# A decoder layer in three-pass fp32r: two chunks of branch B side by side, branch A's inputs loaded sooner, sums of x later in VectorE's order

## The chip, the cores and the metric

One core of a Trainium2 chip runs the whole program in one launch. The metric is the device time in microseconds (us) of that core, as a median over runs. In the profile PE is TensorE (PEld its weight loads), DVE is VectorE, ACT is ScalarE, POOL is GpSimd and SP is SyncE, the engine that issues the DMAs here.

## The reference

The kernel computes one layer of a hybrid decoder for 1024 positions of width 1024 (f32), and a final norm. Cut to the shape of it (the gains and the head reshapes left out):

```python
x = x + 0.5 * swiglu_1(rms(x))                  # width 2816
h = rms(x)
q, f, i, og, pool, gate_a, gate_b = split(h @ w_in)
o   = hgrn2(q, f, i)                            # 8 heads, chunkwise recurrence
y_a = (rms_per_head(o) * silu(og)) @ w_branch_a       # branch A, 1024 x 1024
m   = pool_means(pool) - pool, through pool_w and a scale   # windows 2, 4, 8, 16
y_b = m @ w_branch_b                                  # branch B, 512 x 1024
y   = sigmoid(gate_a) * y_a + sigmoid(gate_b) * y_b
x = x + y @ w_out
x = x + 0.5 * swiglu_2(rms(x))
x = x + sigmoid(rms(x) @ w_ple_gate) * rms(p @ w_ple)
out = rms(x)
```

The change touches the three products with w_branch_b, w_branch_a and w_out.

## The kernel before

**Products.** Every operand of a product is split in two fp32r numbers, hi (cast on ACT, L120) and lo (the remainder, subtracted on DVE, L121). `mm3` issues three matmuls for each product: hi by hi (L159), lo by hi (L160) and hi by lo (L161), each 128x512 into one PSUM bank. The large products go by a seven-product scheme on quarters of the matrices, so operands are also sums and differences of quarters: of weights on POOL (L90, L93), of activations on DVE (L84).

**Order.** A tile framework orders the instructions of each engine ahead of time from the traced program. Within an engine the order is then fixed, and an instruction that waits holds all behind it. `load` (L151) and `store` (L155) are DMAs, all issued by SP, in its order. `behind[0]` names an SP instruction that every load traced from then on is put behind, on SP; `latest[0]` is the load or store traced last. PSUM has tags with 3 (pA), 1 (pB), 1 (pC) and 3 (aux) banks; SBUF tiles come from tagged pools, so that a tile can be written only when the one that had its place has been read.

**Branch B.** `branch_b(j)` makes rows chunk j of y_b: it loads 512 columns' weights rw, splits them to wb, loads the gate gb, does 12 matmuls for each half of the positions into a pA bank (named yb), multiplies by the gate on DVE (L87) and stores to yb_dram. Chunk 0 is done earlier, among the heads; chunks 1 to 7 come here, one after another. Their right operands mh and ml (`m_parts`, four groups of the pool channels) stay in the tag "a" until the last chunk has read them.

**Branch A.** `load_act(i)` loads a quarter of branch A's input (o_dram) as two tiles b1 and b2 and splits it into the operands x0, x3, xT1 and xT3; the tiles lie in the tag "a", too. It is called behind chunks 1, 3, 5 and 7 of branch B. The loop over j = 0, 2, 4, 6 then runs `out_pair`: it loads two quarters of weights, ra and rb, makes wah/wal from ra, wsh/wsl and wth/wtl from sums of both, and wd, and does the seven products. `done` loads a gate and a part of y_b into gy, multiplies, adds, and stores y to y_dram.

**Output product.** `tok` runs over items (product i, half q), with the sides made ahead of the item that uses them: the left operands y (from y_dram) two items ahead, the right ones wo (weights rB, or stored differences rT, rN) four ahead. When a product is done, `read` adds its four banks to x on DVE (L81). Afterwards the norm of the second feed-forward block squares the rows of x on ACT (L220).

Of the kernel before, what the change touches and what calls it, by code (L numbers as in the profile page):

```python
# [16 lines left out]
P = 128  # L17
# [3 lines left out]
KC = D // P  # L21
# [16 lines left out]
def hybrid_block(ctx: ExitStack, tc: tile.TileContext, a: dict, out: bass.AP):  # L38
# [47 lines left out]
    def mul(o, x, y):  # L86
        nc.vector.tensor_tensor(o, x, y, ALU.mult)  # L87
# [414 lines left out]
    ORDER = (1, 2, 5, 6, 3, 7, 4)  # L502
    TOK_TAGS = ("pA", "pA", "pA", "pB"), ("pC", "aux", "aux", "aux")

    def tok(items, lhs, rhs, read, between={}, ahead=2):

# [2 lines left out]
        def operands(of, i, qs):  # L511
            return sum((of(i, q) for q in (qs if isinstance(qs, tuple) else (qs,))), [])

        sides = {lhs: ([], 2), rhs: ([], ahead)}

        def trace(of, at):
            if at < len(items):
                sides[of][0].append(operands(of, *items[at]))

        for at in range(ahead):  # L520
            for of, (_, n) in sides.items():
# [2 lines left out]
        for at, (i, q) in enumerate(items):  # L524
# [6 lines left out]
            for j in range(4):  # L531
                if start:
                    banks[line][j] = bank(TOK_TAGS[line][j])
                ps = banks[line][j]
                c = slice(j * P, (j + 1) * P)
                for k, ((ah, al), (bh, bl)) in enumerate(zip(ls, rs)):
                    mm3(ps, ah[:, c], al[:, c], bh, bl, start and k == 0, last and k == len(ls) - 1)
                if last:
                    read(i, j, ps)
            if (i, q) in between:  # L540
                between[i, q]()

# [647 lines left out]
    def branch_b(j):  # L1190
        r = load(t_("w", "rw")[:, :HALF], a["w_branch_b"][j])
        wh, wl = hilo_half(r, "w", "wb")
        for half, cols in enumerate((L, R)):
# [6 lines left out]
            mul(gb, ps, gb)  # L1200
            store(yb_dram[j][half], gb)

    with tc.manual_schedule(engines={nc.tensor.engine}):
        for h in range(HEADS):
            its = more[h]() if h in more else (v_pair(h + 1), qf_pair(h + 1), og_pair(h + 1))
            among(its, head(h), (66 if h == 7 else 3 * PAIR + 9 * (h in (0, 2))))
        while turns:
            turns.pop(0)()
    behind[0] = og_last[0]

    act_a = new_act()

    def load_act(i):

        b1, b2 = t_("q", "b1"), t_("q", "b2")
        for b, half in ((b1, 0), (b2, 1)):
            for c, at in ((L, 2 * i), (R, 2 * i + 1)):
                load(b[:, c], o_dram[at][half])
        b11, b21, b12, b22 = b1[:, L], b1[:, R], b2[:, L], b2[:, R]

        def put(names, hl):
# [9 lines left out]
        sub(b21, b21, b22)  # L1231
        put(("T1", "N4"), hilo(b1, "a", "xT1"))
        put(("T3", "T2"), hilo(b2, "a", "xT3"))

    for j in range(1, KC):
        steps(branch_b(j))
        if j % 2:
            load_act(j // 2)
    behind[0] = latest[0]


# [68 lines left out]
    def read(i, j, ps):  # L1310
# [8 lines left out]
    rows_2, go_2 = to_next(2)  # L1319
    tok([(i, q) for q in range(2) for i in (1, 2)] + [(i, q) for i in ORDER[2:] for q in range(2)],  # L1320
        *tok_sides(y_of, a["w_out"], wo_dram), read,
        {(3, 1): lambda: rows_2(x), (7, 1): lambda: go_2(x)}, 4)
    act = rest_of(x)
    behind[0] = None

# [174 lines left out]
```

## Time and profile before

| what | value |
|---|---|
| median of 3 runs | 2363.16 us (2357.85 to 2366.03) |
| the profiled execution's own time | 2363.49 us |
| span of the profiled execution | 2361.8 us |
| mean granted clock | 0.992 of full speed |
| TensorE busy | 2312.1 us, 98% |
| VectorE busy | 1469.4 us, 62% |
| ScalarE busy | 983.9 us, 42% |
| GpSimd busy | 447.1 us, 19% |

Times inside the program are counted from the start of the span, so the profiled execution has 1.7 us outside of it. The granted clock is the share of TensorE's full clock (2.4 GHz) that the chip gave it; 0.50 is the lower level, 1.2 GHz. The number in square brackets at the end of a timeline row is how long the engine stood idle ahead of that instruction, and what ended the idle time.

### The profile page before, as it was taken

What the parts mean: (1) busy time and instruction counts of PE and PEld (TensorE: products, weight loads), DVE (VectorE), ACT (ScalarE), POOL (GpSimd) and SP (SyncE); (2) the same over time, 40 slices, a digit from 0 to 9 for tenths busy, and PEclk for the clock granted to TensorE, in tenths of its full rate; (3) what the DMA queues carried; (4) which work ended last, traced back from release to release, by engine and by line L of the source; (5) the groups of instructions that cost most, each with busy time, mean ns of one, the idle gap of its engine ahead of it and who ended that gap; (6) DMA issues with size and microseconds to landing.
All of it is one profiled execution on the core that took longest, in us unless ns stands there. A gap on an engine that the chain in (4) does not pass through costs nothing.

```text
span 2361.8 us, 29424 instructions
## 1 busy us (share of the span) xinstructions
PE 2312.1 (98%) x11058; PEld 1918.6 (81%) x11058; DVE 1469.4 (62%) x2024; ACT 983.9 (42%) x1536; POOL 447.1 (19%) x387
## 2 busy tenths in 40 slices
PE   8999999999999999999999999999999999999998
PEld 6778888888887888788888887877787888888886
DVE  5655555467657765666566666677555644568457
ACT  6434333333555333334433443337333433334555
POOL 1322222200012132122212202101422232100001
PEclk9999999999999999999999999999999999999999
DMA  4344444483332232232232366752344523664245
GB/s 177 137 151 169 153 174 142 147 339 110 135 112 76 76 104 72 78 106 72 83 100 87 99 206 221 252 223 106 102 161 170 201 93 112 231 241 135 80 165 183
DMA packets 137503, 341.19 MB, mean 144 GB/s; under 512 B 15632, under 2 KB 16656, under 8 KB 137360
## 3 DMA queue, kind: packets, MB, share of 16 engines
q1 hardware_dynamic: 137360, 339.31, 41.4%
q8 instruction: 87, 1.43, 0.3%
q14 instruction: 56, 0.46, 0.1%
HBM read 233.86 MB, written 105.38 MB: 144 GB/s over the span
## 4 chain that ended last, share of the span: by engine, by line
PE 80%; DVE 6%; DMA 5%; issue 4%; POOL 2%; ACT 2%; SPq 1%; POOLq 0%; DVEq 0%; ACTq 0%
PE pA L159 13%; PE pA L161 13%; PE pA L160 13%; PE pB L159 6%; PE pB L161 6%; PE pB L160 6%; PE aux L1035 4%; PE pC L161 3%; PE pC L159 3%; PE pC L160 3%; PE aux L161 2%; PE aux L160 2%; PE aux L159 2%; DMA rb<-in_ffn_w_dram 1%; PE tr L268 1%
## 5 line engine op out<-in xcount | busy, mean ns | idle before, releaser
L90 POOL TENSOR_TENSOR s<-rb 128x512 f32<-128x512 f32 x74 | 99.5, 1345 | 755.6 <-DMA rb<-in_ffn_w_dram 318.5
L121 DVE TENSOR_TENSOR wtl<-rb,wth 128x1024 fp32r<-128x1024 f32 x74 | 90.6, 1225 | 158.3 <-ACT wth L120 158.3
L120 ACT CAST wsh<-s 128x1024 fp32r<-128x1024 f32 x74 | 77.8, 1051 | 224.8 <-POOL s L93 188.4
L93 POOL TENSOR_TENSOR rb<-ra,s 128x512 f32<-128x512 f32 x74 | 97.8, 1322 | 331.8 <-DVE wd L121 331.8
L121 DVE TENSOR_TENSOR wal<-ra,wah 128x1024 fp32r<-128x1024 f32 x74 | 91.6, 1239 | 100.2 <-PE pC L160 64.4
L121 DVE TENSOR_TENSOR wsl<-s,wsh 128x1024 fp32r<-128x1024 f32 x74 | 90.9, 1229 | 100.7 <-ACT wsh L120 100.6
L120 ACT CAST wth<-rb 128x1024 fp32r<-128x1024 f32 x74 | 77.6, 1049 | 180.8 <-POOL rb L93 180.8
L120 ACT CAST gh<-gr 128x1024 fp32r<-128x1024 f32 x84 | 81.9, 981 | 143.7 <-PE aux L160 86.6
L121 DVE TENSOR_TENSOR gl<-gr,gh 128x1024 fp32r<-128x1024 f32 x84 | 95.0, 1134 | 71.7 <-ACT gh L120 68.6
L159 PE MATMUL pA<-xT3h,wth 128*128 128x512 f32 x296 | 117.9, 398 | 5.9 <-ACT g L410 4.6
L159 PE MATMUL pB<-xT1h,wsh 128*128 128x512 f32 x296 | 118.5, 400 | 3.9 <-ACT xT1h L120 1.8
L159 PE MATMUL pA<-x0h,wah 128*128 128x512 f32 x296 | 118.5, 400 | 3.4 <-ACT x0h L120 3.4
L120 ACT CAST wah<-ra 128x1024 fp32r<-128x1024 f32 x74 | 77.6, 1050 | 104.4 <-DMA ra<-in_ffn_w_dram 73.0
L160 PE MATMUL pA<-x0l,wah 128*128 128x512 f32 x296 | 115.9, 391 | 2.4 <-DVE x0l L121 2.4
L159 PE MATMUL pB<-x,wth 128*128 128x512 f32 x296 | 117.2, 396 | 0.1
L160 PE MATMUL pB<-xT1l,wsh 128*128 128x512 f32 x296 | 115.9, 391 | 0.6 <-DVE xT1l L121 0.6
L161 PE MATMUL pA<-x0h,wal 128*128 128x512 f32 x296 | 116.0, 392 | 0.3 <-DVE wal L121 0.3
L159 PE MATMUL pA<-xT1h,wsh 128*128 128x512 f32 x280 | 111.3, 398 | 4.9 <-DVE g L81 2.3
L159 PE MATMUL pC<-x0h,wah 128*128 128x512 f32 x296 | 116.1, 392 | 0.0
L161 PE MATMUL pA<-xT3h,wtl 128*128 128x512 f32 x296 | 116.0, 392 | 0.0
L160 PE MATMUL pA<-xT3l,wth 128*128 128x512 f32 x296 | 116.0, 392 | 0.0
L161 PE MATMUL pB<-xT1h,wsl 128*128 128x512 f32 x296 | 115.9, 392 | 0.0
(387 smaller groups left out, 6558.2 us busy)
## 6 DMA issues: line engine op xcount, KB each, us to landing
ra<-in_ffn_w_dram SPq DMA_DIRECT2D x48, 512.0 KB, 3.6
rb<-in_ffn_w_dram SPq DMA_DIRECT2D x44, 512.0 KB, 3.6
gsS<-gs SPq DMA_DIRECT2D x88, 256.0 KB, 2.1
rB<-in_ffn_w_dram SPq DMA_DIRECT2D x40, 512.0 KB, 6.9
gr<-gsS SPq DMA_DIRECT2D x40, 512.0 KB, 3.3
gsA<-g SPq DMA_DIRECT2D x66, 256.0 KB, 2.0
gr<-gsA SPq DMA_DIRECT2D x30, 512.0 KB, 5.3
ra<-in_w_in_dram SPq DMA_DIRECT2D x28, 512.0 KB, 3.6
```

What stands on the lines that cost most here:

```text
L90: nc.gpsimd.tensor_tensor(o, x, y, ALU.add)
L93: nc.gpsimd.tensor_tensor(o, x, y, ALU.subtract)
L120: split_last[1] = nc.scalar.copy(hi, src).ins
L121: split_last[0] = nc.vector.tensor_tensor(lo, src, hi.bitcast(F32), ALU.subtract).ins
L159: nc.tensor.matmul(ps, ah, bh, start=first, stop=False, **kw)
L160: nc.tensor.matmul(ps, ah, bl, start=False, stop=False, **kw)
L161: nc.tensor.matmul(ps, al, bh, start=False, stop=last, **kw)
L268: nc.tensor.matmul(ps[:, c], x[t][:, kc * P : (kc + 1) * P], diag[:, c], start=True, stop=True)
L1035: nc.tensor.matmul(ps[:m, c, :64], kc[c][:, :m], right, start=True, stop=True)
```

## The change

Three edits. (1) Branch B's chunks 6 and 7 are done by a new function, `branch_b_last`: four banks (three pA and the pB) for the four products of both chunks, and the four groups of inputs taken one by one through all four of them; the products with the gates and the stores come with the last group. Chunks 1 to 5 stay. (2) `load_act` becomes a generator of two parts, the loads and the splits, and a table, `ORDER_A`, says behind which chunk which part of which quarter is traced; the last quarter's loads come behind chunk 4, its splits behind the last chunks. The line `behind[0] = latest[0]` stays as it is. (3) For the output product `tok` makes the left operand three items ahead instead of two, and puts each `read` behind the lo split of the next item's operands in DVE's order.

```diff
--- before.py
+++ after.py
@@ -502,7 +502,7 @@
     ORDER = (1, 2, 5, 6, 3, 7, 4)
     TOK_TAGS = ("pA", "pA", "pA", "pB"), ("pC", "aux", "aux", "aux")
 
-    def tok(items, lhs, rhs, read, between={}, ahead=2):
+    def tok(items, lhs, rhs, read, between={}, ahead=2, left=2, turns_=False):
 
@@ -511,11 +511,13 @@
         def operands(of, i, qs):
             return sum((of(i, q) for q in (qs if isinstance(qs, tuple) else (qs,))), [])
 
-        sides = {lhs: ([], 2), rhs: ([], ahead)}
+        sides = {lhs: ([], left), rhs: ([], ahead)}
+        los = {}
 
         def trace(of, at):
             if at < len(items):
                 sides[of][0].append(operands(of, *items[at]))
+                los.setdefault(at, []).append(split_last[0])
 
         for at in range(ahead):
             for of, (_, n) in sides.items():
@@ -536,7 +538,10 @@
                 for k, ((ah, al), (bh, bl)) in enumerate(zip(ls, rs)):
                     mm3(ps, ah[:, c], al[:, c], bh, bl, start and k == 0, last and k == len(ls) - 1)
                 if last:
-                    read(i, j, ps)
+                    with ExitStack() as turn:
+                        for ins in los.get(at + 1, ()) if turns_ else ():
+                            turn.enter_context(tc.issue_after(ins))
+                        read(i, j, ps)
             if (i, q) in between:
                 between[i, q]()
 
@@ -1200,6 +1205,23 @@
             mul(gb, ps, gb)
             store(yb_dram[j][half], gb)
 
+    def branch_b_last(js):
+
+        parts = []
+        for j in js:
+            r = load(t_("w", "rw")[:, :HALF], a["w_branch_b"][j])
+            hl = hilo_half(r, "w", "wb")
+            for half in range(2):
+                gb = load(t_("u", "gb"), gb_dram[j][half])
+                parts.append((j, half, hl, gb, bank(("pA", "pA", "pA", "pB")[len(parts)], "yb")))
+        for g, i in enumerate((0, 2, 1, 3)):
+            c = slice(i * P, (i + 1) * P)
+            for j, half, (wh, wl), gb, ps in parts:
+                mm3(ps, wh[:, c], wl[:, c], *m_parts[g][half], g == 0, g == 3)
+                if g == 3:
+                    mul(gb, ps, gb)
+                    store(yb_dram[j][half], gb)
+
     with tc.manual_schedule(engines={nc.tensor.engine}):
         for h in range(HEADS):
             its = more[h]() if h in more else (v_pair(h + 1), qf_pair(h + 1), og_pair(h + 1))
@@ -1210,12 +1232,15 @@
 
     act_a = new_act()
 
+    ORDER_A = {1: (0, 0), 2: (1,), 3: (1, 2), 4: (3,), 5: (2,), 7: (3,)}
+
     def load_act(i):
 
         b1, b2 = t_("q", "b1"), t_("q", "b2")
         for b, half in ((b1, 0), (b2, 1)):
             for c, at in ((L, 2 * i), (R, 2 * i + 1)):
                 load(b[:, c], o_dram[at][half])
+        yield
         b11, b21, b12, b22 = b1[:, L], b1[:, R], b2[:, L], b2[:, R]
 
         def put(names, hl):
@@ -1231,11 +1256,16 @@
         sub(b21, b21, b22)
         put(("T1", "N4"), hilo(b1, "a", "xT1"))
         put(("T3", "T2"), hilo(b2, "a", "xT3"))
-
-    for j in range(1, KC):
+        yield
+
+    acts = [load_act(i) for i in range(KC // 2)]
+    for j in range(1, KC - 2):
         steps(branch_b(j))
-        if j % 2:
-            load_act(j // 2)
+        for i in ORDER_A[j]:
+            next(acts[i])
+    branch_b_last((KC - 2, KC - 1))
+    for i in ORDER_A[KC - 1]:
+        next(acts[i])
     behind[0] = latest[0]
 
@@ -1319,7 +1349,7 @@
     rows_2, go_2 = to_next(2)
     tok([(i, q) for q in range(2) for i in (1, 2)] + [(i, q) for i in ORDER[2:] for q in range(2)],
         *tok_sides(y_of, a["w_out"], wo_dram), read,
-        {(3, 1): lambda: rows_2(x), (7, 1): lambda: go_2(x)}, 4)
+        {(3, 1): lambda: rows_2(x), (7, 1): lambda: go_2(x)}, 4, 3, True)
     act = rest_of(x)
     behind[0] = None
 
```

On SP, at the end of branch B, `yb_dram<-gb` are branch B's stores, `ra` and `rb` branch A's weights, `gy` the gates and parts of y_b that `done` reads. Before:

```order
L151 DMA b2_1968_11372<-o_dram7_1_106_233 128x512
L155 DMA yb_dram4_1_148_275<-gb_1938_11212 128x512
L151 DMA ra_1980_11400<-in_w_branch_a_dram 128x1024
L151 DMA gy_1992_11452<-ga_dram0_0_107_234 128x512
L155 DMA yb_dram5_0_149_276<-gb_1942_11234 128x512
L151 DMA gy_1992_11452<-yb_dram0_0_139_266 128x512
L151 DMA rb_1983_11406<-in_w_branch_a_dram 128x1024
L155 DMA yb_dram5_1_150_277<-gb_1944_11251 128x512
L155 DMA yb_dram6_0_151_278<-gb_1957_11298 128x512
```

After, the same stretch of SP:

```order
L155 DMA yb_dram4_1_148_275<-gb_1940_11218 128x512
L155 DMA yb_dram5_0_149_276<-gb_1946_11246 128x512
L155 DMA yb_dram5_1_150_277<-gb_1948_11263 128x512
L155 DMA yb_dram6_0_151_278<-gb_1959_11304 128x512
L155 DMA yb_dram6_1_152_279<-gb_1961_11307 128x512
L155 DMA yb_dram7_0_153_280<-gb_1965_11315 128x512
L155 DMA yb_dram7_1_154_281<-gb_1967_11318 128x512
L151 DMA ra_1980_11400<-in_w_branch_a_dram 128x1024
L151 DMA gy_1992_11452<-ga_dram0_0_107_234 128x512
L151 DMA gy_1992_11452<-yb_dram0_0_139_266 128x512
L151 DMA gy_1994_11498<-ga_dram1_1_110_237 128x512
L151 DMA gy_1994_11498<-yb_dram1_1_142_269 128x512
```

The first ra stood behind the last load of an activation chunk (b2) and one store; now it stands behind all of branch B's stores. The first rb follows right after the last row shown.

On DVE, at the end of branch B, `gb<-yb,gb` are the products with the gates, x0l, x3, xT1l and xT3l splits of branch A's input, `b1` and `b2` its differences, wal, wsl, wtl and wd splits of weights. Before:

```order
L87 TENSOR_TENSOR gb_1963_11337<-yb_1964_11339,gb_1963_11337 128x512
L121 TENSOR_TENSOR xT3l_1954_11290<-b2_1947_11269,xT3h_1953_11289 128x1024
L121 TENSOR_TENSOR wtl_1989_11421<-rb_1983_11406,wth_1988_11420 128x1024
L87 TENSOR_TENSOR gb_1965_11354<-yb_1966_11356,gb_1965_11354 128x512
L121 TENSOR_TENSOR x0l_1970_11378<-b1_1967_11371,x0h_1969_11377 128x1024
L121 TENSOR_TENSOR x3_1971_11381<-b2_1968_11372,x3_1971_11381 128x512
L84 TENSOR_TENSOR b1_1967_11371<-b2_1968_11372,b1_1967_11371 128x512
```

After, the same end:

```order
L121 TENSOR_TENSOR x0l_1970_11378<-b1_1942_11235,x0h_1969_11377 128x1024
L121 TENSOR_TENSOR x3_1971_11381<-b2_1943_11236,x3_1971_11381 128x512
L84 TENSOR_TENSOR b1_1942_11235<-b2_1943_11236,b1_1942_11235 128x512
L84 TENSOR_TENSOR b2_1943_11236<-b2_1943_11236 128x512
L84 TENSOR_TENSOR b2_1943_11236<-b2_1943_11236,b1_1942_11235 128x512
L87 TENSOR_TENSOR gb_1959_11304<-yb_1960_11306,gb_1959_11304 128x512
L87 TENSOR_TENSOR gb_1961_11307<-yb_1962_11309,gb_1961_11307 128x512
L87 TENSOR_TENSOR gb_1965_11315<-yb_1966_11317,gb_1965_11315 128x512
L87 TENSOR_TENSOR gb_1967_11318<-yb_1968_11320,gb_1967_11318 128x512
L84 TENSOR_TENSOR b1_1942_11235<-b1_1942_11235,b2_1943_11236 128x512
L121 TENSOR_TENSOR xT1l_1973_11389<-b1_1942_11235,xT1h_1972_11388 128x1024
L121 TENSOR_TENSOR xT3l_1975_11393<-b2_1943_11236,xT3h_1974_11392 128x1024
```

The last quarter's x0l moved from behind the last product with a gate to ahead of the last four of them.

On DVE, in the output product, `x<-pA`, `x<-pC`, `x<-aux` and `x<-pB` are the sums of `read`, yl the lo splits of the left operands and wol those of the right ones. Before:

```order
L121 TENSOR_TENSOR yl_2128_12240<-s2_2126_12237,yh_2127_12239 128x1024
L81 TENSOR_TENSOR x_2105_12120<-pA_2084_12027,x_2105_12120 128x512
L81 TENSOR_TENSOR x_2106_12129<-pA_2085_12034,x_2106_12129 128x512
L81 TENSOR_TENSOR x_2107_12138<-pA_2086_12041,x_2107_12138 128x512
L121 TENSOR_TENSOR wol_2131_12247<-rB22_2129_12244,woh_2130_12246 128x1024
L81 TENSOR_TENSOR x_2132_12256<-pC_2122_12209,x_2132_12256 128x512
L81 TENSOR_TENSOR x_2133_12265<-aux_2123_12216,x_2133_12265 128x512
L81 TENSOR_TENSOR x_2108_12147<-pB_2087_12048,x_2108_12147 128x512
L121 TENSOR_TENSOR yl_2137_12287<-y_2066_11989,yh_2136_12286 128x1024
```

After, the same place:

```order
L121 TENSOR_TENSOR yl_2121_12206<-s2_2119_12203,yh_2120_12205 128x1024
L121 TENSOR_TENSOR yl_2130_12245<-y_2066_11989,yh_2129_12244 128x1024
L121 TENSOR_TENSOR wol_2124_12213<-rB22_2122_12210,woh_2123_12212 128x1024
L81 TENSOR_TENSOR x_2109_12132<-pA_2087_12034,x_2109_12132 128x512
L121 TENSOR_TENSOR wol_2133_12251<-rB22_2131_12248,woh_2132_12250 128x1024
L81 TENSOR_TENSOR x_2134_12260<-pC_2125_12216,x_2134_12260 128x512
L81 TENSOR_TENSOR x_2110_12141<-pA_2088_12041,x_2110_12141 128x512
L81 TENSOR_TENSOR x_2135_12269<-aux_2126_12223,x_2135_12269 128x512
L121 TENSOR_TENSOR yl_2139_12291<-y_2081_12021,yh_2138_12290 128x1024
```

The next yl and one wol moved ahead of the first sum x<-pA, and the sum x<-pC now follows one x<-pA instead of three.

## Rows read from the trace of the kernel before

**Rows 1.** The page's first part: busy time of each engine, its share of the span, and instructions.

```profile
PE 2312.1 (98%) x11058; PEld 1918.6 (81%) x11058; DVE 1469.4 (62%) x2024; ACT 983.9 (42%) x1536; POOL 447.1 (19%) x387
```

**Rows 2.** Windows: the start of branch A, the output product's stretch, and the middle of branch A. Columns: window, its length, busy time (with instructions) of PE, PEld, DVE, ACT and POOL, granted clock, DMA share, GB/s.

```profile
1446.70:1476.20 29.50, 23.71 (x86) 17.88 (x85) 23.37 (x24) 12.56 (x15) 9.34 (x6) 0.88 0.50 160
1577.65:1587.85 10.20, 7.95 (x27) 5.65 (x26) 10.20 (x12) 0.64 (x1) 0.00 (x0) 0.83 0.00 0
1484.00:1506.00 22.00, 22.00 (x99) 18.22 (x98) 13.74 (x18) 6.65 (x9) 7.02 (x5) 1.00 0.67 224
```

**Rows 3.** PE's timeline at the start of branch A: start, duration, engine, line, operation, operands, shapes, and in brackets the idle time ahead and what ended it.

```profile
1446.56 0.39 PE L161 MATMUL yb<-mh,wb 128*128 128x512 f32 x1
1446.78 0.39 PE L159 MATMUL pA<-x0h,wah 128*128 128x512 f32 x1
...
1453.12 0.51 PE L159 MATMUL pA<-x0h,wah 128*128 128x512 f32 x1 [2.10 <-ACT x0h L120]
1455.17 0.51 PE L160 MATMUL pA<-x0l,wah 128*128 128x512 f32 x1 [1.54 <-DVE x0l L121]
...
1465.71 0.78 PE L160 MATMUL pA<-xT3l,wsh 128*128 128x512 f32 x1 [1.70 <-DVE xT3l L121]
...
1476.26 0.39 PE L159 MATMUL pA<-xT1h,wd 128*128 128x512 f32 x1
```

**Rows 4.** PE's timeline in the output product.

```profile
1577.72 0.39 PE L161 MATMUL pB<-woh,yl 128*128 128x512 f32 x1
1579.36 0.47 PE L159 MATMUL pC<-woh,yh 128*128 128x512 f32 x1 [1.25 <-DVE x L81]
...
1581.60 0.63 PE L161 MATMUL pC<-woh,yl 128*128 128x512 f32 x1 [0.99 <-DVE yl L121]
...
1587.89 0.39 PE L159 MATMUL pC<-woh,yh 128*128 128x512 f32 x1
```

**Rows 5.** DVE's timeline at the end of branch B (a product with a gate, a difference, a split of weights) and at the third pair of branch A (a split, a sum that frees bank pB).

```profile
1453.30 0.68 DVE L87 TENSOR_TENSOR gb<-yb,gb 128x512 f32<-128x512 f32 x1
...
1455.63 0.69 DVE L84 TENSOR_TENSOR b<-b,b 128x512 f32<-128x512 f32 x1
...
1456.96 1.22 DVE L121 TENSOR_TENSOR wal<-ra,wah 128x1024 fp32r<-128x1024 f32 x1
...
1495.33 1.23 DVE L121 TENSOR_TENSOR wal<-ra,wah 128x1024 fp32r<-128x1024 f32 x1 [1.05 <-PE pC L160]
...
1500.94 0.69 DVE L81 TENSOR_TENSOR o<-o,pB 128x512 f32<-128x512 f32 x1 [1.01 <-PE pB L161]
```

**Rows 6.** SP's timeline: loads of branch A's weights (ra, rb), four of branch B's stores, and the first load of the output product's weights rT. The duration is what SP took over the issue, its wait included.

```profile
1434.88 0.42 SPq L151 DMA_DIRECT2D ra<-in_w_branch_a_dram  x1
...
1437.29 0.48 SPq L151 DMA_DIRECT2D rb<-in_w_branch_a_dram  x1
1438.02 12.54 SPq L155 DMA_DIRECT2D yb_dram<-gb  x4
1450.65 0.38 SPq L151 DMA_DIRECT2D ra<-in_w_branch_a_dram  x1
...
1489.92 0.33 SPq L151 DMA_DIRECT2D ra<-in_w_branch_a_dram  x1
...
1534.03 0.40 SPq L151 DMA_DIRECT2D rT<-woT  x1
```

**Rows 7.** The view of branch A's weight tile, 1398 to 1480: from issue to landing, shortest, median, longest.

```profile
DMA to landing us min/median/max: 3.6/4.5/6.6
```

**Rows 8.** ACT's timeline: the casts of the first and the second ra.

```profile
1440.72 1.05 ACT L120 CAST wah<-ra 128x1024 fp32r<-128x1024 f32 x1 [10.49 <-DMA ra<-in_w_branch_a_dram]
...
1454.33 1.05 ACT L120 CAST wah<-ra 128x1024 fp32r<-128x1024 f32 x1 [0.74 <-DMA ra<-in_w_branch_a_dram]
```

**Rows 9.** PE's timeline at another long wait of this trace, ahead of branch A.

```profile
989.02 0.80 PE L160 MATMUL aux<-pb,pwhl 128*128 128x512 f32 x1 [3.86 <-DVE pb L121]
```

**Rows 10.** Windows of one microsecond around that wait; the columns are those of rows 2.

```profile
988.00:989.00 1.00, 0.00 (x0) 0.00 (x0) 1.00 (x3) 0.41 (x1) 0.00 (x0) 0.50 0.40 164
993.00:994.00 1.00, 1.00 (x4) 0.78 (x3) 0.20 (x1) 0.69 (x1) 0.00 (x0) 0.50 0.78 279
994.00:995.00 1.00, 1.00 (x5) 0.76 (x4) 0.00 (x0) 0.46 (x1) 0.00 (x0) 0.64 0.59 234
```

**Rows 11.** POOL's timeline: the first sum of branch A's weights.

```profile
1444.01 1.29 POOL L90 TENSOR_TENSOR s<-rb 128x512 f32<-128x512 f32 x1 [39.71 <-DMA rb<-in_w_branch_a_dram]
```

**Rows 12.** PE's timeline at the third pair of branch A: the first matmul into bank pB after the sum of rows 5.

```profile
1503.46 0.39 PE L159 MATMUL pB<-xT1h,wsh 128*128 128x512 f32 x1
```

**Rows 13.** DVE's timeline in the output product.

```profile
1574.97 0.69 DVE L81 TENSOR_TENSOR x<-pA,x 128x512 f32<-128x512 f32 x1 [2.96 <-PE pA L161]
...
1577.40 1.22 DVE L121 TENSOR_TENSOR wol<-rB,woh 128x1024 fp32r<-128x1024 f32 x1
1578.53 0.69 DVE L81 TENSOR_TENSOR x<-pC,x 128x512 f32<-128x512 f32 x1
...
1580.32 1.22 DVE L121 TENSOR_TENSOR yl<-y,yh 128x1024 fp32r<-128x1024 f32 x1
```

**Rows 14.** ACT's timeline after the output product's first sums: the first square of x.

```profile
1590.18 1.06 ACT L220 ACTIVATE xn<-x 128x1024 f32<-128x1024 f32 x1 [11.89 <-DVE x L81]
```

**Rows 15.** The view of tile rT, 1500 to 1600: from issue to landing, shortest, median, longest.

```profile
DMA to landing us min/median/max: 4.9/6.9/9.2
```

## The prediction

> **What bounds the kernel now.** I read the busy shares first. TensorE (PE) is busy 98% of the span [rows 1], so a change that removes no product can win only where PE stands still, or where it runs at the lower of its two clock levels because it stood still. Then I read the windows around the edited code. From 1484 to 1506, in the middle of branch A, PE is busy for all of the 22.00 us, with 99 matmuls [rows 2]: nothing is to be had there. Two stretches are different. Between branch A's first matmul and the one 84 matmuls later (86 in the window, less the two still running when it opens) the granted clock is 0.88 and PE is busy 23.71 of 29.50 us; at the output product a stretch of 25 matmuls (27 less two) has 0.83 and 7.95 of 10.20 us [rows 2]. Third came PE's timeline in both places, with what each idle stretch waited for.
>
> Place 1, the start of branch A. While PE is fed, one 128x512 matmul starts 0.227 us after the one before (1446.56 to 1446.78 [rows 3]; more exactly 0.2268, over long runs). From 1446.78, 84 matmuls should take 84 x 0.2268 = 19.05 us; the 85th starts at 1476.26, 29.48 later. **10.4 us are lost.** The big waits are 2.10 for x0h, 1.54 for x0l and 1.70 for xT3l, all of the last activation chunk [rows 3]; with two small ones the idle time is 5.8, and the rest is work at the lower clock after the waits.
>
> Place 2, the output product. From 1577.72 to 1587.89 are 25 matmuls, 5.67 us if fed, 10.17 measured: **4.5 us are lost**, 1.25 waiting for a sum of x to free bank pC, 0.99 for yl, the rest at the lower clock [rows 4].
>
> The change can win at most 10.4 + 4.5 = 14.9 us directly. Below is what of it is left.
>
> **The activation chunks and branch B.** Side by side, chunks 6 and 7 still take 96 matmuls, so PE reaches the end of branch B at the same time: last start 1446.56, end about 1446.95. Their inputs were loaded long before, and I cost the reordering at nothing; the cover is PE's own queue of those 96 matmuls (21.8 us), and each microsecond by which an input outran it would be one of PE's. The first group's input is free after a quarter of them, so the last chunk's split of x0 no longer waits for the very end. The new DVE order does x0l, x3 and three differences ahead of the four products with the gates and only xT1l and xT3l behind them. Each product takes 0.68 [rows 5] and the last ends at 1446.95 + 0.68 = 1447.65; one more difference (0.69) and two splits (1.22 each [rows 5]) end near 1451. The three waits of place 1 go.
>
> **What is late next: branch A's own weights.** Before, the first of them, ra, was issued at 1434.88 and rb at 1437.29 [rows 6], among branch B's stores. All loads and stores are issued by SP, in its order. The rows show what a store does to it: four stores of yb held SP for 12.54 us from 1438.02, and the second ra was issued right behind them, at 1450.65 [rows 6]. In the new order all seven last stores of yb stand ahead of the first ra, because the mark that branch A's loads are put behind is now the last store (before, it was the last load of an activation chunk). So ra waits for the last product with a gate.
>
> The Trainium skill, "DMA: Bandwidth & Descriptors", section "Anatomy of one DMA", says that the DMA engines wait on no semaphore and that any such wait happens at the issuing sequencer, ahead of the dispatch. It speaks against this part of the change, and the 12.54 us of [rows 6] agree with it.
>
> The sum: last product done 1447.65; SP issues the last store (about 0.4) and then ra at 1448.05. Landing of these weights took 3.6 to 6.6 us, median 4.5 [rows 7]; the ra issued at 1450.65 was in use by 1454.33 [rows 8], that is 3.7 at most, also behind a store. I take 4.2, nearer to that row than to the longest: landed at 1452.25. The cast wah takes 1.05 [rows 8]: PE's first matmul at 1453.4. The split wal takes 1.22 [rows 5]: from 1454.6 PE has all three products. That third matmul would start at 1446.78 + 0.45 = 1447.2, so PE is 7.4 us late. To this comes the clock. Where PE had waited 3.86 us until 989.02, the granted clock was 0.50 at 988 and still 0.50 at 993, and 0.64 in the microsecond from 994 [rows 9, 10]: about 5.4 us of work at half speed, worth some 2.4 to 2.7. So the new loss is 7.4 + 2.4 = **9.8 against 10.4: a gain of 0.6**. With a landing of 3.6 it is a gain of 1.2, with 6.6 a loss of 1.8.
>
> The same page and section fits a transfer's time as about 2.0 us plus its bytes at 436 GB/s: 3.2 us for these 512 KB, an estimate from that page. The trace has 3.6 at the least [rows 7]; by the fit the sum would come out one microsecond better.
>
> rb follows ra and four loads of gates, at about 1450.2 instead of 1437.29 [rows 6]. Two 1.29 us sums on POOL [rows 11], a cast and a split stand between its landing and its first use: near 1461, when PE, itself late, wants it near 1462. I cost it at 0 (0 to 1).
>
> **Further into branch A.** Each later weight load stands on SP behind a store of y, so it comes later too: the estimated lags of the issues shrink from 13 us (first rb) over 12 and 7 to about 5.4 for the third pair's ra (before: 1489.92 [rows 6]). That one decides: its split wal stood at 1495.33 on DVE, the sum that frees bank pB at 1500.94, and PE entered pB again at 1503.46 [rows 5, 12], a slack of 1.8 behind the sum's end. Now wal comes at about 1500.3 and pushes that sum to end near 1503.9, while PE, 0.6 earlier, wants pB near 1502.8. **A new wait of 1.2** (0 if the lag is smaller by a fifth; 2.5 if the landing is slow and the clock falls).
>
> **The output product.** Left operands are traced one item sooner, and each sum of x goes on DVE behind the splits of the next item. Before, the sums x<-pC stood behind three sums x<-pA that can't run until PE has filled those banks (1574.97, idle 2.96 ahead of it), and behind wol at 1577.40; so x<-pC ran at 1578.53 and the next yl at 1580.32 [rows 13]. Now yl and the first wol come ahead of x<-pA, and the order is x<-pA, wol, x<-pC: 1574.97 + 0.69, + 1.22, + 0.69, hence x<-pC ends at about 1577.5, ahead of the 1577.95 at which PE wants pC. The yl of that item is ready before 1574. Both waits and the slow work behind them go: **4.5 us**. What is late next is ACT's work for the norm, whose first square of x ran at 1590.18 after 11.89 idle [rows 14]; I take off 0.2 for it: **+4.3** (0 to 4.5). Moving the reads costs no instruction; the loads of this product's weights rT are issued some 6 us later than 1534.03 [rows 6], and took 4.9 to 9.2 to land [rows 15], with about 9 us of cover. I cost that at nothing; the cover is the four rights traced ahead, and where it fails each microsecond counts on PE.
>
> **Sum.** 0.6 - 1.2 + 4.3 = 3.7 us. The profiled execution took 2363.49 (1.7 outside the span of 2361.8), 0.3 above the median of 2363.16, so the forecast is 2363.49 - 3.7 = 2359.8. 0.3% (7.1 us) is about what a measurement of this kernel can tell from no change, so this counts as within it.
>
> **Rivals.**
> A. One of the two gains is not had: ra lands in 6.6 (place 1 loses 1.8), or a further sum of x still stands ahead of the one that PE wants. For it: only 0.5 us of slack at x<-pC. That gives 2362 to 2364.5.
> B. Slower: the lag on SP runs through branch A. If an issue lag of 5 to 7 us beats the cover at two of the three later pairs, PE stops twice by about 2.5 and works on at half clock each time, 2 x (2.5 + 2.4) = 9.8 in place of the 1.2 above: 2359.8 + 8.6 = 2368.4. It decides from a lag of about 6 us against a slack of 1.8 plus what DVE can reorder. Against it: at 1484 to 1506 PE never waited [rows 2].
> C. The stores don't hold ra, the change does what its words say, and both losses go, with perhaps 1 us left over: 2363.49 - 13.9 = 2349.6. Against it are the 12.54 us of [rows 6].
> D. PE's clock doesn't fall for long in the one long wait, or the new wait of 1.2 doesn't come, and ra lands in 3.6: 2.4 + 1.2 or 0.6 better, 2355 to 2358.
>
> **How the numbers follow.** Forecast (2358 to 2362): 0.42. A: 0.22. D: 0.14. B: 0.12. C: 0.10. Faster by over 0.3% means below 2356.1: C, and a little under half of D with the near edge of the forecast, 0.20. Slower by over 0.3% means above 2370.3: the worse half of B, 0.07. The rest, 0.73, is within. The range 2353 to 2367 takes in the forecast, A, D and the better half of B, and leaves out C and the worse half of B.
>
> **What would show it.** Right: in the new trace PE waits at the start of branch A once, some 6 to 8 us, for wah or ra and not for x0h, x0l or xT3l; SP issues the first ra right after the last store of yb, near 1448; the granted clock is 0.5 for about five microseconds behind that wait; x<-pC at the output product ends before PE wants it and that stretch has clock 1.0. Wrong: ra issued before 1440 (then C), PE waits above 2 us between 1465 and 1520 (then B), or PE waiting for a sum of x at the output product (then A).

## The result and the profile after

| | median | range | runs |
|---|---|---|---|
| before | 2361.94 us | 2357.85 to 2366.65 | 20 |
| after | 2365.47 us | 2359.01 to 2370.55 | 20 |

The ratio is 1.0016, with a 95% interval of 1.0009 to 1.0022: the change makes the kernel slower, by about 3.5 us. The profiled execution has a span of 2365.2 us, against 2361.8.

The busy shares tell nothing of it. The first part of the page of the changed kernel reads as [rows 1] does:

```profile
PE 2309.9 (98%) x11058; PEld 1916.1 (81%) x11058; DVE 1467.4 (62%) x2024; ACT 984.6 (42%) x1536; POOL 447.5 (19%) x387
```

What tells it is the start of the same matmul in both traces. PE's timeline after the change, with its waits, at the two places of [rows 3] and [rows 4] and between them:

```profile
1446.02 0.39 PE L161 MATMUL yb<-mh,wb 128*128 128x512 f32 x1
1453.96 0.79 PE L159 MATMUL pA<-x0h,wah 128*128 128x512 f32 x1 [7.55 <-ACT wah L120]
...
1475.41 0.39 PE L159 MATMUL pA<-xT1h,wd 128*128 128x512 f32 x1
...
1484.99 0.50 PE L159 MATMUL pB<-xT1h,wsh 128*128 128x512 f32 x1 [1.26 <-DVE o L81]
...
1506.25 0.50 PE L159 MATMUL pB<-xT1h,wsh 128*128 128x512 f32 x1 [1.93 <-DVE o L81]
...
1511.76 0.50 PE L159 MATMUL pA<-xT3h,wth 128*128 128x512 f32 x1 [2.47 <-ACT o L410]
...
1537.52 0.50 PE L159 MATMUL pA<-xT1h,wd 128*128 128x512 f32 x1 [1.20 <-ACT o L413]
...
1585.76 0.39 PE L161 MATMUL pB<-woh,yl 128*128 128x512 f32 x1
1585.99 0.39 PE L159 MATMUL pC<-woh,yh 128*128 128x512 f32 x1
```

Branch B's last matmul stands at 1446.02 here and at 1446.56 before: this execution came 0.54 early to the changed part. At the matmul of 1476.26 before it is 0.85 early (1475.41), at that of 1577.72 it is 8.04 late (1585.76), and the span is 3.4 longer. So:

- place 1, the start of branch A: gained 0.3;
- **from 1476 to 1577, the middle and end of branch A and the lead into the output product: lost 8.9;**
- the output product and what follows: gained 4.6.

At place 1 the waits for x0h, x0l and xT3l are gone, and one wait of 7.55 for wah has come. Between 1476 and 1540 stand four waits that before had not, 6.86 us of idle time. With the slow work behind them they cost 9.4; 0.5 of it comes back near 1561, where PE waited 0.52 for yh before and does not wait now. At the output product x<-pC no longer holds anybody: PE starts its bank 0.23 after the matmul before it, and the window there (columns as in rows 2) has no idle time and the full clock, where [rows 2] have 0.83:

```profile
1580.00:1590.00 10.00, 10.00 (x46) 8.28 (x45) 9.31 (x12) 8.28 (x9) 0.00 (x0) 1.00 0.00 0
```

SP's timeline shows the weight loads, in the places of [rows 6]:

```profile
1433.81 13.67 SPq L155 DMA_DIRECT2D yb_dram<-gb  x6
1447.54 1.24 SPq L151 DMA_DIRECT2D ra<-in_w_branch_a_dram  x1
...
1450.76 0.38 SPq L151 DMA_DIRECT2D rb<-in_w_branch_a_dram  x1
...
1454.28 0.33 SPq L151 DMA_DIRECT2D ra<-in_w_branch_a_dram  x1
1466.99 0.32 SPq L155 DMA_DIRECT2D y_dram<-o  x1
...
1468.39 0.38 SPq L151 DMA_DIRECT2D rb<-in_w_branch_a_dram  x1
...
1484.37 0.32 SPq L155 DMA_DIRECT2D y_dram<-o  x1
...
1485.26 0.40 SPq L151 DMA_DIRECT2D rb<-in_w_branch_a_dram  x1
...
1497.56 0.33 SPq L151 DMA_DIRECT2D ra<-in_w_branch_a_dram  x1
```

The first ra comes right behind six stores of yb that hold SP for 13.67 us, as was reckoned; that a wait sits at the issuing sequencer (the Trainium skill, "DMA: Bandwidth & Descriptors", section "Anatomy of one DMA") agrees with it. The first rb is 13.5 late against [rows 6]. But the second and the third rb come late as well, each behind a store of y that waits for its sums: 1468.39 and 1485.26. In the kernel before they were

```profile
1454.91 0.39 SPq L151 DMA_DIRECT2D rb<-in_w_branch_a_dram  x1
...
1476.45 0.33 SPq L151 DMA_DIRECT2D rb<-in_w_branch_a_dram  x1
```

How a late rb reaches PE is read from four engines. First POOL, whose sums of weights need rb, and whose last one of a pair is the last reader of an older ra:

```profile
1496.25 1.29 POOL L93 TENSOR_TENSOR rb<-ra,s 128x512 f32<-128x512 f32 x1 [1.84 <-DVE wd L121]
1507.14 1.66 POOL L90 TENSOR_TENSOR s<-rb 128x512 f32<-128x512 f32 x1 [9.60 <-DMA rb<-in_w_branch_a_dram]
```

The sum of 1496.25 ends at 1497.54, and SP issues the fourth ra at 1497.56: the tile that ra is to take came free then. Next DVE and ACT:

```profile
1502.45 1.22 DVE L121 TENSOR_TENSOR wal<-ra,wah 128x1024 fp32r<-128x1024 f32 x1 [1.18 <-ACT wah L120]
...
1505.52 0.68 DVE L81 TENSOR_TENSOR o<-o,pB 128x512 f32<-128x512 f32 x1
```

```profile
1510.17 1.04 ACT L120 CAST wsh<-s 128x1024 fp32r<-128x1024 f32 x1 [7.76 <-POOL s L93]
1511.13 0.58 ACT L410 COPY o<-pA 128x512 f32<-128x512 f32 x1
```

That ra's split wal stands on DVE at 1502.45 (1495.33 in [rows 5]), and four operations on, the sum that frees pB ends at 1506.20: PE's wait of 1.93. On ACT the copy that frees a pA bank stands behind the cast wsh, which waits 7.76 for POOL's sums of the fourth rb: PE's wait of 2.47. Neither bank was late by its own work; each stood behind a weight operation. The fourth wait, 1.20 at 1537.52, is of the same kind one stage on: the copy that frees its bank stands on ACT behind a cast of the output product's weights (woh), which waited 5.34 for the load of rB.

In the trace of before, the copy that is at 1511.13 here stood behind the same cast, on ACT:

```profile
1503.54 1.05 ACT L120 CAST wsh<-s 128x1024 fp32r<-128x1024 f32 x1 [7.45 <-POOL s L93]
1504.49 0.58 ACT L410 COPY o<-pA 128x512 f32<-128x512 f32 x1
```

and PE entered that bank at

```profile
1506.18 0.39 PE L159 MATMUL pA<-xT3h,wth 128*128 128x512 f32 x1
```

The copy ended at 1505.07, so the slack was 1.1 us.

### The profile page after: what moved, and what is told of

The parts are those of the page before. It is cut to its first block, busy times and chain, and to the rows that moved or that the text cites. A ratio compares the mean times of both kernels' runs of the same rounds, so it can differ in the third digit from the quotient of the medians.

```text
span 2365.2 us, 29421 instructions
## 1 busy us (share of the span) xinstructions
PE 2309.9 (98%) x11058; PEld 1916.1 (81%) x11058; DVE 1467.4 (62%) x2024; ACT 984.6 (42%) x1536; POOL 447.5 (19%) x387
## 4 chain that ended last, share of the span: by engine, by line
PE 81%; DVE 5%; issue 4%; DMA 4%; POOL 3%; ACT 2%; SPq 0%; POOLq 0%; DVEq 0%; ACTq 0%
PE pA L159 13%; PE pA L161 13%; PE pA L160 13%; PE pB L159 6%; PE pB L161 6%; PE pB L160 6%; PE aux L1040 4%; PE pC L159 3%; PE pC L161 3%; PE pC L160 3%; PE aux L160 3%; PE aux L161 3%; PE aux L159 3%; DMA rb<-in_ffn_w_dram 1%; POOL s L90 1%
## 5 line engine op out<-in xcount | busy, mean ns | idle before, releaser
L159 PE MATMUL pB<-x,wth 128*128 128x512 f32 x296 | 117.2, 396 | 0.1
L160 PE MATMUL pB<-x,wth 128*128 128x512 f32 x296 | 115.4, 390 | 0.4 <-DVE x L121 0.4
```

The lines of the kernel that those rows point to most:

```text
L159: nc.tensor.matmul(ps, ah, bh, start=first, stop=False, **kw)
L160: nc.tensor.matmul(ps, ah, bl, start=False, stop=False, **kw)
```

## The experiments

The theory after the result: branch A's first weights are held by the stores (that was in the forecast), and the middle is late because later weight loads stand on SP behind stores of y. The rival: the side-by-side order itself delays branch A, four products with gates and four stores coming at its end. Each run was taken beside runs of before of its own, whose medians are 2362.41 us (e1 to e4), 2363.22 (e5 to e8) and 2361.16 (e9 to e12); each ratio is to these.

**The mark, in both kernels (e1, e2), and the parts (e3, e4).** Edit of e1, on the changed kernel; `loaded[0]` is the DMA that `load` issued last:

```diff
-    behind[0] = latest[0]
+    behind[0] = loaded[0]
```

> The changed kernel with one line different: branch A's loads are put behind the last load of branch B, not behind its last store. Theory (the stores hold the first weights on SP, and the lag then runs through all of branch A): the wait for wah goes (7.5 us and the slow work behind it), the four waits in the middle of branch A go (6.9 us of idle time and the slow work behind them), the output product keeps its gain: about 2346 to 2351 us. Rival (the side-by-side order itself delays branch A, since four products with gates and four stores come at its end): the wait for wah goes but most of the 9 us in the middle of branch A stays: 2355 to 2359.

Measured: 2360.46 us, ratio to before 0.9992 (0.9981 to 1.0002). Both expectations missed it, the theory by over 9 us, the rival by 1.5. PE's waits from 1440 to 1640 (engine, bank, line, what was waited for: us in total, times, longest):

```profile
PE pA L159 <- DVE o L81: 3.7, 2, 3.2
PE pA L159 <- DVE gb L87: 3.3, 1, 3.3
PE tr L268 <- PE pC L161: 0.8, 1, 0.8
PE pA L159 <- ACT o L413: 0.7, 1, 0.7
PE pB L159 <- DVE o L81: 0.4, 1, 0.4
```

The wait for wah is gone, and two new long ones have come. DVE's timeline at the end of branch B and SP's two later loads show where they are from:

```profile
1445.91 1.23 DVE L121 TENSOR_TENSOR wsl<-s,wsh 128x1024 fp32r<-128x1024 f32 x1 [2.27 <-ACT wsh L120]
...
1448.86 2.48 DVE L87 TENSOR_TENSOR gb<-yb,gb 128x512 f32<-128x512 f32 x4
```

```profile
1479.55 0.42 SPq L151 DMA_DIRECT2D rb<-in_w_branch_a_dram  x1
...
1492.40 0.33 SPq L151 DMA_DIRECT2D ra<-in_w_branch_a_dram  x1
```

The four products with gates, now in one group, stand behind the split wsl of the early weights and what follows it; PE waits 3.3 us for the first of them, which frees its bank. And PE, 6.1 us ahead of before near 1475, has no lead left near 1502: the third rb comes at 1479.55, later than the 1476.45 of before, though PE is ahead. So the rival was right on a price at branch B's end; the middle asked for an experiment of its own.

Edit of e2, on the kernel before; `stored[0]` is the DMA that `store` issued last:

```diff
-    behind[0] = latest[0]
+    behind[0] = stored[0]
```

> The kernel before with the mark alone changed: branch A's loads put behind branch B's last store, nothing side by side, output product as before. Theory: the start of branch A loses about the same as before (the wait for wah covers those for x0h and x0l), and the waits in the middle of branch A appear, some 9 us: about 2369 to 2373 us. Rival (side-by-side order makes the loss): within 2 us of before, 2360 to 2364.

Measured: 2367.65 us, 1.0024 (1.0014 to 1.0034). Without anything side by side, its longest PE waits from 1375 to 1640 are those of the changed kernel:

```profile
PE pA L159 <- ACT wah L120: 6.4, 1, 6.4
PE pB L159 <- DVE o L81: 3.7, 2, 2.6
PE pA L159 <- ACT o L413: 2.0, 2, 1.3
PE pA L159 <- ACT o L410: 1.4, 1, 1.4
```

So the mark alone makes a loss, and the rival that the side-by-side order makes it falls. The loss is 5.2 us in the medians, less than the 7 to 11 expected. In its trace the start and the middle of branch A take 8.0 more than before; 1.6 comes back at the output product, where the same two waits (1.3 and 1.0) left the granted clock at 1.00, while before it was 0.50 from 1582 to 1585.

e3 and e4 part the output product from the rest. e3 gives the kernel before the new `tok` and its call; e4 takes them from the changed kernel:

```diff
-        {(3, 1): lambda: rows_2(x), (7, 1): lambda: go_2(x)}, 4, 3, True)
+        {(3, 1): lambda: rows_2(x), (7, 1): lambda: go_2(x)}, 4, 2, False)
```

> The kernel before with the output product's part of the change alone (left operands three ahead, sums of x behind the next splits). Theory: both waits at that place go with the slow work behind them, 4.5 to 5 us: 2357 to 2358 us. Rival (the stretch looks better only because it came later in the changed kernel, its weights long landed): 0 to 2 us of gain, 2360 to 2362.

> The changed kernel without the output product's part. Theory: its gain of 5 us is missing, 2369 to 2372 us. Rival: 2365 to 2367.

Measured: e3 2357.76 us, 0.9979 (0.9971 to 0.9987); e4 2370.28 us, 1.0031 (1.0021 to 1.0041). The output product's part is worth 4.7 us on the one side (2362.41 - 2357.76) and 4.8 on the other (2370.28 - 2365.47; 4.3 if each is taken against its own runs of before).

**One load (e5), and the same load the other way (e6).** e5 is the kernel before; the step that loads and sums the third pair's rb is put behind two stores of y on SP:

```diff
-        steps(out_pair(a["w_branch_a"][j], a["w_branch_a"][j + 1], act_a, done))
+        it = out_pair(a["w_branch_a"][j], a["w_branch_a"][j + 1], act_a, done)
+        steps(it, 1)
+        with ExitStack() as turn:
+            if j == 4:
+                for at in ((2, 0, 0), (0, 1, 0)):
+                    turn.enter_context(tc.issue_after(stored[at]))
+            steps(it, 1)
+        steps(it)
```

> The kernel before with one load moved: the third pair's rb (issued at 1476.45 before) is put behind the next two stores of y on SP, nothing else is asked for. Theory (the waits in the middle of branch A come from this load: its landing sets the sums on POOL, these free the tile for the fourth pair's ra, and ra's split stands on DVE ahead of the sum that frees a bank): rb some 6 to 8 us later, PE waits 2 to 5 us between 1500 and 1512 and works slowly behind it: 2366 to 2370 us. Rival (the middle is late only because branch A began late): within 1.5 us of before, 2361 to 2364.

Measured: 2365.66 us, 1.0013 (1.0005 to 1.0022), 2.4 us above its runs of before: the interval leaves out no change, and it is a little less than the theory expected. Its SP and PE rows (this kernel's lines are numbered one higher):

```profile
1480.96 1.52 SPq L151 DMA_DIRECT2D rb<-in_w_branch_a_dram  x1
...
1493.66 0.33 SPq L151 DMA_DIRECT2D ra<-in_w_branch_a_dram  x1
```

```profile
PE pA L160 <- ACT o L411: 2.1, 1, 2.1
```

rb came 4.5 us later than the 1476.45 of before, the ra that needs the tile of its sums 3.7 later than in [rows 6], and PE waited 2.1 for a copy on ACT, the wait that is 2.47 in the changed kernel, with slow work behind it.

e6 is e1 with that rb traced in the second pair's first `done`, ahead of its store; the store is put behind it:

```diff
+            if (j, i, half) == (2, 0, 0):
+                raws[4] = load(t_("w", "rb"), a["w_branch_a"][5])
...
+                    turn.enter_context(tc.issue_after(raws["ins"]))
                 store(y_dram[j + i][half], t)
```

> The kernel of e1 (mark at the last load of branch B) with the third pair's rb put ahead of the two stores of y that stand ahead of it there, as it was in the kernel before. Theory: the wait of 3.25 us near 1499 goes with the slow work behind it, 5 to 6 us: 2353 to 2356 us. Rival (branch A's middle is bounded by something else, so a lead of 6 us is given back wherever it comes from): 2358 to 2361.

Measured: 2358.69 us, 0.9982 (0.9972 to 0.9991). The wait of 3.25 went, yet the gain over e1 is 1.8 us in the medians (2.6 if each is taken against its own runs of before), and the intervals overlap: the rival's number. In its trace PE was 6.1 us ahead of before near 1470 and 1.0 near 1530; four waits of 0.5 to 1.4 us stand between. The third rb alone is not the whole of it.

**The products with gates (e7), and not side by side (e8).** e7, on the kernel of e6, puts the first pair's splits of weight sums behind the last product with a gate on DVE:

```diff
+        if j == 0:
+            steps(it, 1)
+            with tc.issue_after(gated):
+                steps(it, 1)
```

> The kernel of e6 with the splits of the first pair's weight sums (wsl, wd, wtl) put behind the last product with a gate on DVE, so that the four products at the end of branch B run as soon as their banks are full. Theory: the wait of 3.27 us for a gate product at branch A's start goes too, and the slow work behind it: 2348 to 2352 us. Rival (the splits, now later, hold PE instead): as e6 or slower.

Measured: 2357.43 us, 0.9978 (0.9969 to 0.9987), not to be told from e6: inconclusive. The wait for a product with a gate fell only from 3.3 to 2.6, so the split wsl was not the whole of that price.

e8 is the changed kernel with e1's mark and without `branch_b_last`: chunks 6 and 7 go one after the other.

> The kernel before with the output product's part and the sooner loads of branch A's inputs, but with chunks 6 and 7 one after the other, and the mark at the last load. Theory (the last quarter's splits still wait for the end of branch B, so place 1 stays; the mark and the third rb are as before): 2356 to 2359 us, as e3. Rival (the sooner loads alone take the waits of place 1 away): 2348 to 2352.

Measured: 2356.69 us, 0.9978 (0.9968 to 0.9988), as expected, within what e3 gives. Its PE still waits 1.5 for x0l and 1.7 for xT3l: the sooner loads alone take neither wait away. In e1, which has the side-by-side order too, both are gone.

**Both late loads (e9, e10).** e9 is the changed kernel with its mark as it is; the second and the third rb are traced as in e6:

```diff
+    raws, early = {}, {(0, 0, 0): 2, (2, 0, 0): 4}
...
+            n = early.get((j, i, half))
+            if n:
+                raws[n] = load(t_("w", "rb"), a["w_branch_a"][n + 1])
+                raws["ins"] = latest[0]
```

> The changed kernel, its mark left at the last store, with the second and the third pair's rb put ahead of the stores of y that they stood behind on SP. Theory (the late second and third rb make the 9 us in the middle of branch A, the late first ra makes only the start): the first wait for wah stays at 7 to 8 us, of the 9.4 us in the middle at least 5 go: 2357 to 2361 us. Rival (the whole chain is shifted by the late first ra, so the order behind it doesn't matter): 2363 to 2366.

Measured: 2359.47 us, 0.9988 (0.9977 to 0.9998), 6.0 less than the changed kernel. Its PE waits from 1440 to 1640, all of them:

```profile
PE pA L159 <- ACT wah L120: 9.3, 1, 9.3
PE tr L268 <- PE pC L161: 0.8, 1, 0.8
```

The first wait stays and the four others are gone. The second and the third rb, at 1468.39 and 1485.26 in the changed kernel, now come at

```profile
1454.32 0.33 SPq L151 DMA_DIRECT2D rb<-in_w_branch_a_dram  x1
...
1476.86 0.33 SPq L151 DMA_DIRECT2D rb<-in_w_branch_a_dram  x1
```

The windows of the middle, first of the changed kernel, then of e9 (the columns are those of rows 2):

```profile
1476.00:1540.00 64.00, 57.14 (x242) 45.80 (x241) 38.65 (x48) 19.49 (x25) 12.79 (x10) 0.97 0.66 224
```

```profile
1476.00:1540.00 64.00, 63.88 (x281) 52.19 (x280) 45.78 (x54) 20.43 (x25) 12.42 (x9) 1.00 0.77 263
```

39 matmuls more in the same 64 us, 39 x 0.2268 = 8.8 us: the loss in the middle. Two loads, each behind a store that waits, make it. The median gains less than that, 6.0 (5.2 if each is taken against its own runs of before): in this execution the first ra took 6.5 us from its issue (1446.51) to its cast (1452.97), 5.3 in the changed kernel, and the start of branch A took 2.6 us longer.

e10 is e7 with both loads early:

> The kernel of e7 with the second rb too put ahead of the store of y that it stood behind. Theory (a weight load behind a store of y costs its wait at every pair): the wait near 1480 goes, 1 to 3 us less than e7: 2354 to 2356.5 us. Rival (the second pair's loads still stand behind branch B's last stores and the tiles of the pool are full, so PE's lead of 6 to 8 us is given back whatever their order): 2356.5 to 2359, as e7.

Measured: 2354.95 us, 0.9969 (0.9958 to 0.998), the lowest ratio of all; its interval overlaps those of e3, e7 and e8. The lead of 5.0 us near 1471 is still 5.2 at 1561. What is left are two longer waits, 2.5 for a product with a gate and 1.5 for a sum.

What holds the products with gates here, 1449.10 for the first of them, is a row of DVE and the rows of ACT that it waited for (lines are numbered two higher):

```profile
1447.16 0.69 DVE L123 TENSOR_TENSOR x<-b,x 128x512 fp32r<-128x512 f32 x1 [1.08 <-ACT x L122]
```

```profile
1445.56 1.05 ACT L122 CAST wsh<-s 128x1024 fp32r<-128x1024 f32 x1 [4.85 <-POOL s L95]
1446.52 0.61 ACT L122 CAST x<-b 128x512 fp32r<-128x512 f32 x1
```

The split x3 of branch A's input stands on DVE ahead of the four products; its cast stands on ACT behind wsh, and wsh waited 4.85 for POOL's sums of weights. No run tried another order there.

**The two halves of the output product's part (e11, e12)**, on the kernel before: left operands three ahead only, and sums behind the splits only:

```diff
-        {(3, 1): lambda: rows_2(x), (7, 1): lambda: go_2(x)}, 4)
+        {(3, 1): lambda: rows_2(x), (7, 1): lambda: go_2(x)}, 4, 3, False)
```

```diff
-        {(3, 1): lambda: rows_2(x), (7, 1): lambda: go_2(x)}, 4)
+        {(3, 1): lambda: rows_2(x), (7, 1): lambda: go_2(x)}, 4, 2, True)
```

> The kernel before with only the left operands of the output product made three items ahead; the sums of x are not tied to the splits. Theory (yl then stands ahead of the sums, but x<-pC still behind three x<-pA and two wol): the wait for yl goes, that for x<-pC stays or grows: 2360 to 2362 us. Rival (the operands sooner are the whole gain): 2357 to 2358.5.

> The kernel before with only the sums of x put behind the next item's splits; left operands two items ahead as before. Theory (x<-pC then stands ahead of the three x<-pA): the wait for x<-pC goes and, with the yl behind two sums only, most of that for yl: 2357 to 2359 us. Rival (without the sooner operands the sums wait for splits that come late): 2361 to 2364.

Measured: e11 2362.46 us, 1.0009 (0.9999 to 1.0019); e12 2358.48 us, 0.999 (0.9979 to 1.0). The sooner operand alone makes the wait for x<-pC longer; PE's longest wait from 1440 to 1640 in e11 is

```profile
PE pC L159 <- DVE x L81: 3.0, 1, 3.0
```

since a second wol now stands ahead of that sum. The order of the sums is what gains. That the operands add to it, together with it, is likely but not shown: e12's trace keeps a wait of 0.7 for x<-pC that e3's has not, but the intervals of e3 and e12 overlap.

**The stretches in all traces.** The start is the time from the start of branch B's last matmul to that of the 85th matmul of branch A (before: 1446.56 to 1476.26). The middle is the time from there to the 337th (before: 1476.26 to 1533.60). It is one execution each, read from PE's timelines:

| kernels | start, us | middle, us |
|---|---|---|
| before | 29.7 | 57.3 |
| e3, e8, e11, e12 (chunks 6 and 7 in turn, mark at a load) | 27.1 to 28.4 | 57.8 to 58.8 |
| e5 (third rb late) | 27.8 | 62.1 |
| after; e4 (as after, without the output product's part) | 29.4; 28.4 | 66.8; 65.7 |
| e2 (mark alone) | 28.7 | 66.4 |
| e9 (as after, both rb sooner) | 32.0 | 57.9 |
| e1, e6, e7 (side by side, mark mended) | 23.4 to 24.4 | 62.5 to 65.2 |
| e10 (as e7, both rb sooner) | 24.2 | 57.8 |

Where both rb come in time, the middle takes 57.3 to 58.8; where both come late, 65.7 to 66.8. The side-by-side order gains 3 to 5 us at the start once the mark is mended, and e10 keeps it. That the whole kernel gains by it is not told from the noise of the medians (e8 and e10 overlap).

## Why the prediction was wrong

The forecast was 2359.8 us within 2353 to 2367, a gain of 3.7; measured is a loss of 3.5. The measured 2365.47 lies in that range, but on the side of rival B: the direction was wrong. Step by step, on the profiled execution:

| step | forecast | measured |
|---|---|---|
| place 1, start of branch A | +0.6 | +0.3 |
| further into branch A | -1.2 | -8.9 |
| output product | +4.3 | +4.6 (4.7 in e3) |
| sum | +3.7 | -4.0, with 0.5 of lead from ahead of the change -3.4 |

**Place 1** was right in its mechanism. The three waits went, the first ra was issued at 1447.54 (forecast 1448.05), and PE started at 1453.96 (1453.4). The landing was slower (1447.54 to the cast at 1452.86 is 5.3, the forecast had 4.2), but the split wal, which the forecast had PE wait for, cost about 0.2. From PE's start the 84 matmuls took 2.4 us more than when fed (21.45 against 19.05), as forecast.

That the size came out is partly luck. The 10.4 us lost before were read from one execution, and its start of 29.7 is the longest of the six with that order; by the others 1.3 to 2.6 us less were to be had. The 3.2 us that the prediction worked out for the landing come from a fit that the Trainium skill ("DMA: Bandwidth & Descriptors", section "Anatomy of one DMA") gives for DMAs issued by GpSimd; these are issued by SP, and no run here shows it for them.

**The output product** was right too: x<-pC ran ahead of the moment at which PE wanted the bank, and the stretch has clock 1.00. The first load of rT came at 1547.74, 13.7 us later than before and not 6, and PE waited for none of these weights.

**The step that failed is "Further into branch A. A new wait of 1.2".** The mechanism was named, that each later weight load stands behind a store of y; the term was mis-sized, 8.9 against 1.2, in three ways. The lags were taken to shrink from 13 over 12 and 7 to 5.4; they were 13.5, 13.5 and 8.8 for the three rb, and 7.6 for the ra of 1489.92 (the prediction calls it the third pair's; it is the fourth's), since a late rb keeps POOL's sums late and those keep the next ra's tile. One bank was followed, pB at the third pair, and there the wait was 1.93, near the 1.2; but PE stopped at three more places, 4.9 us in all, two of them at banks freed by copies on ACT behind casts of weights, which the forecast didn't look at. And its sum counted no slow work behind these waits; that was 2.6. The new order on SP had the third rb two stores later than before, and that was read as a lag that shrinks, not as a place in the queue: e5 shows the price of that one place, e9 that the late second and third rb make the 8.9.

**Rival B** was this case, and its sign came, a PE wait above 2 us between 1465 and 1520 (2.47): it has 9.8 for the waits in the middle and 2368.4 us. Its 9.8 is near the measured 9.4 partly by luck: it has two waits of 2.5 with slow work behind both, and there were four, with 1.7 of the 2.6 us of slow work behind one of them. It got a chance of 0.12 because PE never waited from 1484 to 1506 in the trace of before. That row shows that the supply was in time there, not how much in time; the slack of 1.8 at one bank was the hint, and it was smaller than every lag in the sum. At the bank of the longest new wait the slack was 1.1.

That the result is slower by 0.16% lies inside what the text called within 0.3%; with 20 runs a side it is told from no change all the same.

**Why the mended mark gave less than its waits (e1).** The mark was the cause of the loss against before, but a lead is kept only if the loads further on come sooner as well. In e1 the third rb stood behind stores of y and came at 1479.55. In e6 and e7 it came at 1474.10 and 1471.58, but the second rb at 1458.15 and 1458.95, and PE's lead still ran into waits. Only e10, with the second rb at 1455.96 and the third at 1470.67, kept it. The side-by-side order, which the forecast cost at nothing, has a price of its own there: 2.5 to 3.3 us of waiting for a product with a gate in e1, e6, e7 and e10. In the changed kernel the wait for wah covers it.

## What to carry to other kernels

Where one queue issues loads and stores in order, a mark that says "behind the last DMA" must be looked at when the last DMA changes from a load to a store: the load then waits for the store's data. And a row in which the bottleneck engine never waits gives no slack: before a supply is made later, or a lead is hoped for, follow the chain of each load (landing, sums, the tile that they free, casts and splits in order, the bank behind them) and compare every lag with the smallest slack on it.

## What the runs showed of the hardware

The single runs of the kernel before, all with the same program, spread from 2354.84 to 2369.5 us, and they go with the mean granted clock: the runs at 0.997 took 2356.8 us on the mean, those at 0.995 2360.9, those at 0.993 2363.4 and those at 0.991 2365.9 (101 runs, beside the three groups of experiments; 2, 31, 15 and 4 of them have these clocks). A difference of 2.5 us is thus what two runs of one program 0.002 apart in granted clock can show (0.995 and 0.993), and a median of three runs was 1.2 us off that of twenty (2363.16 and 2361.94).

The granted clock fell behind the two longest new waits, as in [rows 10]. Behind the wait of 7.55 it was 0.50, the lower level, until 1457 and 1.00 from 1458. Behind the wait of 2.47 at 1511.76 it was 0.50 from 1513 to 1515 and 1.00 from 1516; a matmul took 0.63 us from 1512.65 on, against 0.39 ahead of it:

```profile
1512.09 0.39 PE L160 MATMUL pA<-xT3l,wth 128*128 128x512 f32 x1
1512.32 0.53 PE L161 MATMUL pA<-xT3h,wtl 128*128 128x512 f32 x1
1512.65 0.63 PE L159 MATMUL pA<-xT3h,wth 128*128 128x512 f32 x1
```

Behind the waits of 1.26 and 1.20 the clock stayed at 1.00. Four idle waits of 6.86 us in all thus cost 9.4 in the middle. What a wait costs also differs between executions: the two waits at the output product, 1.25 and 0.99 in before and 1.3 and 1.0 in e2, were followed by a clock of 0.50 in the one and 1.00 in the other.
